# A hybrid decoder layer: the opening's VectorE and DMA work put into program order, later norms begun earlier, adaLN rows double-buffered and spread over the work, two spreads moved ahead of the FFN

## The chip, the cores and the metric

The kernel runs on one core of a Trainium2 chip. The time is device microseconds of one execution; the median of three runs of the kernel before is 2461.54 us (2461.07 to 2465.44). One more execution was profiled. The core has five engines with a queue each: TensorE (PE, with its weight loads PEld), VectorE (DVE), ScalarE (ACT), GpSimd (POOL) and SyncE (SP), whose queue issues every DMA here. Each queue is worked in order: an instruction that waits for a semaphore holds up all that stand behind it.

## The reference

One layer of a decoder with 2048 tokens and width 1024, all in float32:

```
mod = silu(c) @ w_ada + b_ada                        # adaLN: six vectors of 1024
shift1, scale1, gate1, shift2, scale2, gate2 = split(mod, 6)
h = rmsnorm(x, norm1_w) * (1 + scale1) + shift1
q, k, v, z, xbc, dt = split(h @ w_in)
a = sliding_window_attention(rope(q), rope(k), v, sinks)     # 8 heads, window 128
xbc = silu(causal_depthwise_conv(xbc, conv_w, conv_b))
y = ssd_chunked_scan(xbc, softplus(dt + dt_bias), A, ...)     # Mamba-2, chunks of 128
y = rmsnorm_by_group(y * silu(z)) * ssm_norm_w
x = x + gate1 * (concat(a, y) @ w_out)
h = rmsnorm(x, norm2_w) * (1 + scale2) + shift2
g, u = split(h @ w_gate_up);  x = x + gate2 * ((silu(g) * u) @ w_down)   # width 2816
out = rmsnorm(x, final_norm_w)
```

## The kernel before

A float32 product is made of three matmuls: each operand is split into a part `hi`, rounded to the matmul's type, and the rest `lo`, and hi·hi, hi·lo and lo·hi are summed in a PSUM bank (`mm3`, L231 to L234). So each weight and each activation that goes into a product is first split: `hi` on ScalarE, `lo` on VectorE or GpSimd (`weight`, L213; `split`). Weights of the mixer that are used in four blocks are split once and their halves stored in HBM and read again (L228, L220).

Tokens come in 4 blocks of 512 (b = 0 to 3). Activations are held with the width on the partitions, 8 tiles of 128 x 512. The layer runs in two phases. The mixer phase takes each block through `queries`, `keys_values`, `convolved` and `gated` (projections with 24 to 48 dense matmuls between two `yield`s; one such stretch is called a piece here), and `out_proj` for blocks 0 and 1. The FFN phase first multiplies two blocks at a time by the gate and up weights (`quad`, seven products instead of eight from sums of operands, which `operands` prepares), then `down`.

Between the pieces, side work is let in. `beside` calls `tick(ratio)` after each piece of the main work; each tick adds the ratio to a counter, and for each whole unit the first generator in `sides` makes one step: attention and the state-space scan of an earlier block. MIX, 1.2, is that ratio from block 1 on, and 0.5 holds in block 0 and at the end. `pending` holds things to be done after so many ticks. `finish` runs a side's remaining steps without dense work between them.

The norm of the next block is `norm1`: eight tiles of x are loaded, squared on ScalarE and added up on GpSimd (L242), then the column sums are made on TensorE (L247), the root on VectorE (`rstd`, `rsqrt`), the root is spread to all partitions by a matmul with ones (`spread`, L260), x is loaded a second time and multiplied with it (`modulated`, L265 to L268). `norm_ahead` starts this, and puts the sums 8 ticks and the spread 12 ticks later. For block 0 `first_norm` (L920) keeps x in SBUF, adds its squares on VectorE, and then multiplies out 16 rows of adaLN (`ada`: a row of 128 x 1024 is loaded and reduced against silu(c) on VectorE, L153). The rotary tables (`rope_tables`, L172) stand before it in the program.

The other 32 rows of adaLN are done in halves of 128 x 512 through one buffer `aw` (`ada_halves`, L155): load, reduce (L159), load the second half, reduce. `with_ada` lets in two rows for three pieces, from `convolved` of block 0 until `convolved` of block 1.

The order on TensorE is the program's own within the mixer phase (`manual_schedule`). On all other engines, and on SP's queue, a planner puts the instructions in an order by the times that it estimates; buffers come from pools with a fixed number each (`t` 9, `hl` 12, `raw` 5, `w` 6), and a load into a used buffer waits until the last reader is done.

## Time and profile before

| | |
|---|---|
| median of 3 runs | 2461.54 us (2461.07 to 2465.44) |
| the profiled execution: its time, its span | 2463.36 us, 2461.7 us |
| TensorE busy | 2246.5 us of the span, 91% |
| VectorE, GpSimd, ScalarE busy | 1439.6, 1255.0 and 967.5 us |
| mean granted TensorE clock | 0.963 |
| DMA | 403.81 MB, mean 164 GB/s |
| first dense matmul, keys and values of block 0, convolved of block 1 | 50.5, 80.0 and 265 us |
| first matmul of the FFN, the FFN without stalls | 813.8, from 861 us |

The span runs from the first to the last instruction. A row of the page's groups or of the waits names the engine, the tile and the line, and what ended the wait: "PE d L247 <- POOL t L242" is a matmul of L247 that waited for GpSimd's L242. The line of an operation can be a helper's. The granted clock falls where TensorE has been idle, and matmuls after an idle stretch take longer.

### The profile page before, as it was taken

The numbers are of one execution on the slowest core, as the hardware profiler recorded it, in microseconds if no ns is written. First come the engines' busy times: TensorE is split into PE (matmuls) and PEld (weight loads), VectorE is DVE, ScalarE is ACT, GpSimd is POOL, SyncE is SP. The second block draws the span as 40 slices with busy tenths as digits, with TensorE's granted clock in tenths as the row PEclk, the third lists the DMA queues.
The fourth block names the chain that finished last, engine by engine and source line by source line (L and its number), as shares of the span: only waits on it lengthen the run. The fifth ranks groups of instructions, "written<-read, shape, count | busy, mean of one in ns | idle before, by whom it ended". The sixth has DMA issues, their size and how long they took to land.

```text
span 2461.7 us, 32964 instructions
## 1 busy us (share of the span) xinstructions
PE 2246.5 (91%) x11198; PEld 1877.8 (76%) x11198; DVE 1439.6 (58%) x2526; ACT 967.5 (39%) x2004; POOL 1255.0 (51%) x1249
## 2 busy tenths in 40 slices
PE   1969789899899699999999998899799999999996
PEld 1859678787788488888888787687588888878785
DVE  8456775774334976555765533538855555554554
ACT  3444542574136543445433422224333333333332
POOL 2755633554111698654786333226766666643432
PEclk9979999999899799999999999899899999999998
DMA  5778867867876233222334654664322222263451
GB/s 228 246 266 272 297 221 246 287 221 258 272 232 195 88 116 99 82 69 86 99 99 128 217 181 152 234 205 150 133 98 77 83 85 90 78 219 99 139 163 52
DMA packets 244456, 403.81 MB, mean 164 GB/s; under 512 B 21952, under 2 KB 68032, under 8 KB 244288
## 3 DMA queue, kind: packets, MB, share of 16 engines
q1 hardware_dynamic: 243136, 400.66, 49.8%
q8 instruction: 88, 1.44, 0.2%
q10 hardware_dynamic: 1152, 1.05, 0.1%
q14 instruction: 80, 0.66, 0.1%
HBM read 307.19 MB, written 94.44 MB: 163 GB/s over the span
## 4 chain that ended last, share of the span: by engine, by line
PE 73%; DVE 7%; DMA 6%; ACT 2%; issue 1%; POOL 1%; SPq 0%; DVEq 0%; POOLq 0%; ACTq 0%
PE d L233 10%; PE d L234 10%; PE d L232 10%; PE d L794 9%; PE d L796 8%; PE d L795 8%; DMA aw<-in_wada_dram 4%; PE am L232 1%; PE am L233 1%; PE am L234 1%; DVE aw L159 1%; DVE b L770 1%; PE sm L673 1%; PE st L794 1%; PE st L796 1%
## 5 line engine op out<-in xcount | busy, mean ns | idle before, releaser
L742 ACT ACTIVATE w<-raw 128x512 fp32r<-128x512 f32 x308 | 193.8, 632 | 530.2 <-PE d L234 264.3
L794 PE MATMUL d<-b,w 128*128 128x512 f32 x924 | 373.9, 405 | 19.2 <-ACT b L769 9.4
L795 PE MATMUL d<-b,w 128*128 128x512 f32 x924 | 370.1, 401 | 1.8 <-DVE b L770 1.8
L796 PE MATMUL d<-b,w 128*128 128x512 f32 x924 | 368.9, 399 | 1.8 <-DVE w L743 1.8
L232 PE MATMUL d<-a,w 128*128 128x512 f32 (+1 forms) x720 | 280.3, 396 | 15.9 <-ACT a L862 9.6
L233 PE MATMUL d<-a,w 128*128 128x512 f32 (+1 forms) x720 | 282.1, 392 | 2.7 <-DVE a L737 2.7
L234 PE MATMUL d<-a,w 128*128 128x512 f32 (+1 forms) x720 | 282.2, 392 | 0.0
L743 POOL TENSOR_TENSOR w<-raw,w 128x512 fp32r<-128x512 f32 x88 | 118.7, 1349 | 296.2 <-ACT w L742 277.7
L743 POOL TENSOR_TENSOR w<-s,w 128x512 fp32r<-128x512 f32 x132 | 189.7, 1437 | 136.2 <-ACT w L742 123.0
L873 DVE SCALAR_TENSOR_TENSOR x<-d,mod,x 128x512 f32<-128x512 f32 (+1 forms) x182 | 131.0, 725 | 182.1 <-PE d L234 178.8
L743 DVE TENSOR_TENSOR w<-raw,w 128x512 fp32r<-128x512 f32 x220 | 194.6, 885 | 69.6 <-ACT w L742 66.9
L794 PEld LDWEIGHTS d<-b,w 128*128 128x128 f32 x924 | 175.9, 190 | 61.8 <-ACT b L769 10.9
L796 PEld LDWEIGHTS d<-b,w 128*128 128x128 f32 x924 | 176.3, 191 | 42.7 <-DVE w L743 2.3
L795 PEld LDWEIGHTS d<-b,w 128*128 128x128 f32 x924 | 176.5, 191 | 40.8 <-DVE b L770 3.8
L232 PE MATMUL d<-w,hl 128*128 128x256 f32 (+1 forms) x640 | 186.9, 292 | 2.0 <-ACT hl L267 1.6
L234 PE MATMUL d<-w,hl 128*128 128x256 f32 (+1 forms) x640 | 183.7, 287 | 3.7 <-DVE hl L268 3.7
L233 PE MATMUL d<-w,hl 128*128 128x256 f32 (+1 forms) x640 | 184.1, 288 | 0.0
L232 PEld LDWEIGHTS d<-a,w 128*128 128x128 f32 x720 | 136.5, 190 | 51.0 <-ACT a L862 12.1
L242 POOL TENSOR_TENSOR t<-t 128x512 f32<-128x512 f32 (+1 forms) x84 | 106.8, 1272 | 128.6 <-ACT t L241 121.7
L225 POOL TENSOR_TENSOR w<-raw,w 128x512 fp32r<-128x512 f32 (+1 forms) x72 | 98.3, 1373 | 129.6 <-ACT w L224 109.1
L233 PEld LDWEIGHTS d<-a,w 128*128 128x128 f32 x720 | 136.7, 190 | 36.1 <-DVE a L737 4.3
L234 PEld LDWEIGHTS d<-a,w 128*128 128x128 f32 x720 | 136.2, 189 | 30.7 <-issue 0.2
(311 smaller groups left out, 5418.4 us busy)
## 6 DMA issues: line engine op xcount, KB each, us to landing
raw<-in_wgu_dram SPq DMA_DIRECT2D x176, 256.0 KB, 2.7
raw<-in_wd_dram SPq DMA_DIRECT2D x176, 256.0 KB, 2.7
w<-w_x SPq DMA_DIRECT2D x48, 512.0 KB, 5.3
w<-w_o SPq DMA_DIRECT2D x48, 512.0 KB, 4.5
act<-t SPq DMA_DIRECT2D x88, 256.0 KB, 2.1
t<-act SPq DMA_DIRECT2D x88, 256.0 KB, 4.5
t<-in_xT_dram SPq DMA_DIRECT2D x80, 256.0 KB, 4.6
aw<-in_wada_dram SPq DMA_DIRECT2D x64, 256.0 KB, 3.5
```

The lines of the kernel that those rows point to most:

```text
L159: nc.vector.tensor_tensor_reduce(w, w, csil[:, hs], 0.5, (part if half else b_ada)[:, i:i + 1], ALU.mult, ALU.add, (mod if half else part) ...
L225: nc.gpsimd.tensor_tensor(lo, raw[:, :n], hi.bitcast(F32), ALU.subtract)
L232: nc.tensor.matmul(out, ahi, bhi, start=first, stop=False)
L233: nc.tensor.matmul(out, ahi, blo, start=False, stop=False)
L234: mm3.last = nc.tensor.matmul(out, alo, bhi, start=False, stop=last)
L242: eng.tensor_tensor(acc, acc, sq, ALU.add)
L742: nc.scalar.activation(hi, x, AF.Copy)
L743: eng.tensor_tensor(lo, x, hi.bitcast(F32), ALU.subtract)
L794: nc.tensor.matmul(out, ahi, bhi, start=first and k == 0, stop=False, skip_group_check=True)
L795: nc.tensor.matmul(out, ahi, blo, start=False, stop=False, skip_group_check=True)
L796: mm3.last = nc.tensor.matmul(out, alo, bhi, start=False, stop=k == 3, skip_group_check=True)
L873: nc.vector.scalar_tensor_tensor(x, ps, gate2[:, c:c + 1], x, ALU.mult, ALU.add)
```

## The change

The opening's VectorE, TensorE and SP instructions are put in program order (`manual_schedule` over `silu_c`, `first_norm` and `rope_tables`). In that order the norm comes first, its squares are summed by TensorE itself, each of block 0's eight tiles is modulated as soon as its two adaLN rows are there, six of the query weights are loaded between, and the rotary tables come last. The other 32 adaLN rows have two buffers `aw`; a row's two loads are issued, and its reductions come three ticks later (`ada_later`), one step at each tick, beginning with `keys_values` of block 0. The norm of block 1 is begun after `queries` of block 0, that of block 2 before `queries` of block 1, that of block 3 before `convolved` of block 2, with their sums 16 or 17 and their spreads 21 or 22 ticks later. `out_proj` of blocks 0 and 1 load and split their operands some pieces earlier (`take(out, 2)`). The attention of block 2 begins beside `keys_values` of block 3. The spreads for the FFN's first `operands` are made before `gated` of block 3, in two other banks. MIX is 1.1. In the FFN phase the attention of block 3 comes before both scans.

On VectorE in the opening there stood, in the middle of the rotary table's steps (L182 to L185) and the root (L193 to L205) of block 0's norm:

```order
L153 ISA m_352,mod<-m_352,csil,vec 128x1024
L153 ISA mod 128x1
L183 SCALAR_TENSOR_TENSOR s<-s 128x512
L194 TENSOR_SCALAR rstd<-rsq 128x4
L932 SCALAR_TENSOR_TENSOR scl_151<-mod,vec 128x1
L184 SCALAR_TENSOR_TENSOR s<-s 128x512
L204 TENSOR_TENSOR rsq<-rstd 128x4
L185 SCALAR_TENSOR_TENSOR s<-s 128x512
L205 SCALAR_TENSOR_TENSOR rsq<-rsq,ms 128x4
```

Now the root is done in one go, and after it each tile of the operand `hl` follows its two rows, with a reduction of a later adaLN row (`aw`, L165) ahead of each of its two passes:

```order
L154 ISA m_357,mod<-m_357,csil,vec 128x1024
L154 ISA mod 128x1
L948 SCALAR_TENSOR_TENSOR scl_145<-mod,vec 128x1
L165 ISA aw,part<-aw,csil,vec 128x512
L165 ISA part 128x1
L274 SCALAR_TENSOR_TENSOR t<-m_229,scl_145,at 128x512
L165 ISA aw,mod<-aw,csil,part 128x512
L165 ISA mod 128x1
L277 SCALAR_TENSOR_TENSOR hl<-t,mod,hl 128x512
```

The rows of adaLN are no longer between the root's steps; the tables have moved behind the eighth such group, and 20 halves of later rows stand ahead of the first rotary product.

In SP's queue the first reading of block 1's x (L273) stood between the weights of `convolved` (`in_wx`), the stores of their halves (L228) and other traffic (numbers behind a name tell its uses apart):

```order
L273 DMA t_903<-in_xT_dram 128x512
L228 DMA w_x_3_1_1183<-w_1178 256x1x512
L223 DMA raw_1479<-in_wx_dram 128x512
L393 DMA xs0_203<-sx_984 128x512
L478 DMA m1_2964<-kv3_190 128x256
L228 DMA w_x_4_0_1251<-w_1246 256x1x512
L223 DMA raw_1504<-in_wx_dram 128x512
L228 DMA w_x_4_1_1270<-w_1265 256x1x512
L393 DMA xs0_203<-sx_1063 128x512
L223 DMA raw_1562<-in_wx_dram 128x512
L273 DMA t_908<-in_xT_dram 128x512
```

Now it is over before the first of these stores, and adaLN loads stand between:

```order
L229 DMA raw_1042<-in_wx_dram 128x512
L282 DMA t_728<-in_xT_dram 128x512
L160 DMA aw_2322<-in_wada_dram 128x512
L160 DMA aw_2536<-in_wada_dram 128x512
L282 DMA t_733<-in_xT_dram 128x512
L160 DMA aw_2537<-in_wada_dram 128x512
L282 DMA t_738<-in_xT_dram 128x512
L160 DMA aw_2869<-in_wada_dram 128x512
L282 DMA t_743<-in_xT_dram 128x512
L160 DMA aw_2870<-in_wada_dram 128x512
L360 DMA q0_149<-m2_673 128x512
```

The x loads have moved up past 13 weights of `convolved`, and 21 halves of adaLN have come ahead of the last of them. Up to the first reloaded weight of block 1's `convolved`, SP now issues 77.1 MB with all 64 halves of `aw`, where before it issued 64.9 MB with 22 of them (counted from the shapes in the order).

The diff, cut to its core:

```diff
-MIX, RATIO_UP = 1.2, 0.6
+MIX, RATIO_UP = 1.1, 0.6
-    common, extra = tiles(sb, M1, M2, M4), tiles(xp, 4, 10, 4)
+    common, extra = tiles(sb, M1, M2, M4), tiles(xp, 3, 10, 4)
...
-    def ada_halves(i):
-        for half in range(2):
-            w, hs = big("aw", 1, pool=ip), slice(half * T, (half + 1) * T)
+    def ada_later(i):
+        halves = [slice(0, T), slice(T, D)]
+        ws = [big("aw", 2, pool=ip) for _ in halves]
+        for w, hs in zip(ws, halves):
             nc.sync.dma_start(w, wada[i, :, hs])
-            nc.vector.tensor_tensor_reduce(w, w, csil[:, hs], 0.5, (part if half else b_ada)[:, i:i + 1],
-                                           ALU.mult, ALU.add, (mod if half else part)[:, i:i + 1])
+        for _ in range(3):
+            yield
+        m, pt = mod[:, i:i + 1], part[:, i:i + 1]
+        for w, hs, src, dst in zip(ws, halves, (b_ada[:, i:i + 1], pt), (pt, m)):
+            nc.vector.tensor_tensor_reduce(w, w, csil[:, hs], 0.5, src, ALU.mult, ALU.add, dst)
+        yield
...
-    def operands(s, ops, bp, banks):
-
-        bc = [spread(y_of[2 * s + j], bc=banks[j]) for j in range(2)]
+    def operands(s, ops, bp, bc):
...
     def first_norm():
-        accs, h, x0 = [tmp(), tmp()], [], []
+        st, h, x0, ws = side_bank(0), [], [], []
         for d in range(KT):
             x = extra.m2()
             x0.append(x)
             last_load = nc.sync.dma_start(x, xT[0, d])
-            square_into(accs[d % 2], x, d < 2, nc.vector)
-        acc = accs[0]
-        nc.vector.tensor_tensor(acc, acc, accs[1], ALU.add)
-        bc = spread(rstd(acc, st=side_bank(0)), bc=side_bank(1))
+        for d in range(2):
+            ada(8 + d, common.m4)
+            ada(d, extra.m4)
         for d in range(KT):
-            ada(8 + d, common.m4)
+            sq = tmp()
+            nc.scalar.activation(sq, x0[d], AF.Square)
+            for t in range(NT):
+                nc.tensor.matmul(st[:, 2 * t:2 * t + 2], sq[:, t * P:(t + 1) * P], ones[:, 0:2],
+                                 start=d == 0 and t == 0, stop=d == KT - 1 and t == NT - 1, skip_group_check=True)
+        y = root_of(st, NT)
+        bc = spread(y, bc=side_bank(1))
+        ada(10, common.m4)
+        for d in range(KT):
             nc.vector.scalar_tensor_tensor(scl1[:, d:d + 1], mod[:, 8 + d:9 + d], 1.0, n1w[:, d:d + 1],
                                            ALU.add, ALU.mult)
-            ada(d, extra.m4)
             h.append(modulated(x0[d], bc, scl1[:, d:d + 1], sh1[:, d:d + 1], operand()))
-        return h, last_load
-
-    rope_tables()
-    h, last_load = first_norm()
+            if d + 2 < KT:
+                ada(2 + d, extra.m4)
+            if d + 3 < KT:
+                ada(11 + d, common.m4)
+            if d % 2 == 0 and d < 6:
+                ws.append([weight(wq[c][d // 2], 512, (f"q{c}", d // 2), False) for c in range(2)])
+        return h, last_load, ws
+
+    with tc.manual_schedule(engines={mybir.EngineType.PE, mybir.EngineType.DVE, mybir.EngineType.SP}):
+        for i in range(2):
+            silu_c(i)
+        h, last_load, first_ws = first_norm()
+        rope_tables()
...
     def tick(ratio):
...
+        if ada_rest:
+            next(ada_rest[0], None)
...
-        pending.extend([[8, lambda: next(g)], [12, lambda: next(g)]])
+        pending.extend([[n, lambda: next(g)] for n in at])
...
         run(queries(0, h), 0)
+        with tc.issue_after(last_load.ins):
+            nxt = norm_ahead(1, (17, 21))
+        rest = rest_of_ada()
+        ada_rest.append(rest)
         run(keys_values(0, h), 0)
...
+        nxt = norm_ahead(2, (16, 22))
+        run(queries(1, h), MIX)
...
+        nxt = norm_ahead(3, (16, 22))
         run(convolved(2, h), MIX)
         finish(mix0)
         out = out_proj(0, y_of, lambda c: operand(), lambda c: dense())
-        nxt = norm_ahead(3)
-        run(gated(2, h), MIX)
-        next(out)
-        next(out)
+        g = gated(2, h)
+        take(g, 4)
+        for _ in range(4):
+            tick(MIX)
+        take(out, 2)
+        run(g, MIX)
         run(out, MIX)
         h = nxt
         run(queries(3, h), MIX)
-        run(keys_values(3, h), MIX)
+        out = out_proj(1, y_of, lambda c: operand() if c % 2 else halved(extra.m4()), lambda c: dense())
         finish(mix1)
+        sides.append(attentions(2, common))
+        take(out, 2)
+        run(keys_values(3, h), 0.5)
         prepared(3)
...
         run(out, 0.5)
         run(convolved(3, h), 0.5)
+        bcs = [spread(y_of[b], bc=side_bank(2 + b)) for b in range(2)]
         run(gated(3, h), 0.5)
+        drain(rest)
         finish(sides[0] if sides else None)
...
+    sides.extend([attentions(3, common), ssds(2, stepping[2], common), ssds(3, stepping[3], common)])
...
-        drain(operands(0, ops, bp, [dense(), dense()]))
+        drain(operands(0, ops, bp, bcs))
```

54 lines of the change are left out of this document (17 added, 37 removed).

## The prediction

> **What bounds the kernel now.** I read the page first, then the waits of TensorE, the stretches by stage, the timeline of the opening, the adaLN tile `aw`, and last the order of both programs. The page:
>
> ```profile
> span 2461.7 us, 32964 instructions
> PE 2246.5 (91%) x11198; PEld 1877.8 (76%) x11198; DVE 1439.6 (58%) x2526; ACT 967.5 (39%) x2004; POOL 1255.0 (51%) x1249
> ...
> PE 73%; DVE 7%; DMA 6%; ACT 2%; issue 1%; POOL 1%; SPq 0%; DVEq 0%; POOLq 0%; ACTq 0%
> ```
>
> TensorE is busy for 91% of the span and carries 73% of the chain that ended last. The change adds no dense matmul and removes none, so it can only win what TensorE idles, 2461.7 - 2246.5 = 215 us, and the slow matmuls that follow idling. Where that lies, by stage (the columns are busy us and count of PE, PEld, DVE, ACT and POOL, the granted TensorE clock, the DMA share and its GB/s; the rows are four pieces of the opening, convolved of block 0, the rest up to convolved of block 1, that and the rest of its phase, the middle of the mixer, its end, and the start of the FFN):
>
> ```profile
> 10.00:15.00 5.00, 0.00 (x0) 0.00 (x0) 5.00 (x10) 4.50 (x7) 0.00 (x0) 1.00 1.05 406
> 35.00:40.00 5.00, 0.00 (x0) 0.00 (x0) 5.00 (x11) 1.15 (x2) 1.29 (x1) 1.00 0.88 327
> 45.00:50.00 5.00, 2.08 (x2) 0.50 (x2) 4.11 (x11) 0.29 (x1) 0.00 (x0) 1.00 0.00 0
> 80.00:85.00 5.00, 4.57 (x38) 4.38 (x37) 3.46 (x11) 2.36 (x4) 5.00 (x7) 1.00 0.41 121
> 92.50:176.50 84.00, 57.78 (x236) 46.39 (x235) 51.48 (x123) 43.71 (x95) 51.80 (x54) 0.82 0.85 296
> 176.50:265.30 88.80, 80.48 (x637) 78.98 (x636) 58.82 (x160) 40.73 (x108) 49.48 (x67) 0.96 0.85 287
> 265.30:350.30 85.00, 67.81 (x338) 56.34 (x337) 60.12 (x141) 44.20 (x103) 37.12 (x51) 0.90 0.75 245
> 447.20:659.10 211.90, 202.85 (x1261) 179.79 (x1258) 122.83 (x301) 101.73 (x251) 93.78 (x141) 0.98 0.77 255
> 805.00:861.00 56.00, 33.48 (x131) 24.60 (x130) 54.31 (x76) 32.39 (x73) 38.44 (x26) 0.70 0.29 90
> 861.00:1362.00 501.00, 501.00 (x2444) 417.21 (x2442) 315.80 (x466) 219.44 (x489) 350.78 (x339) 1.00 0.32 98
> ```
>
> From 861 to 1362 TensorE never stops: nothing is to be had there. What the change can reach lies before 861. Who ended the long waits:
>
> ```profile
> PE d L247 <- POOL t L242: 32.3, 2, 19.3
> PE at L260 <- DVE t L258: 27.1, 1, 27.1
> PE am L247 <- DVE t L928: 17.9, 1, 17.9
> ...
> PE d L232 <- ACT m L210: 9.4, 1, 9.4
> ...
> PE at L491 <- DMA m<-q: 4.8, 1, 4.8
> ...
> PE d L260 <- DVE t L258: 3.7, 1, 3.7
> ```
>
> The first row is the norms of blocks 1 and 2: TensorE stood at their column sums until GpSimd had added the last square. The two longest single waits are the opening's own norm. The 9.4 us are the first matmul of the second output projection, which waits for its operand to be split.
>
> **The opening, +4 us (from -8 to +14).** VectorE sets the pace there (5.00 of 5.00 us busy in the pieces at 10 and at 35, while DMA, at 406 GB/s first, has nothing left at 45). The new order lets TensorE begin as soon as the first pair of operands is there, but it puts two things ahead of the rotary tables: 12 of the 16 first adaLN rows with the modulation, and 20 halves of *later* adaLN rows. The durations:
>
> ```profile
> 15.25 0.69 DVE L185 SCALAR_TENSOR_TENSOR s<-s 128x512 f32<-128x512 f32 x1
> ...
> 22.02 0.43 DVE L181 TENSOR_SCALAR s<-s 128x512 f32<-128x512 f32 x1
> ...
> 23.70 1.28 DVE L153 CUSTOM_DVE_ANT_0 m<-m,csil,vec 128x1024 f32<-128x1024 f32 x1
> ...
> 24.39 7.78 POOL L225 TENSOR_TENSOR w<-raw,w 128x512 fp32r<-128x512 f32 x5 [18.68 <-DMA raw<-in_wq_dram]
> ...
> 24.90 1.49 DVE L182 TENSOR_SCALAR s<-s 128x512 f32<-128x512 f32 x1
> ...
> 48.93 5.36 DVE L265 SCALAR_TENSOR_TENSOR t<-m,scl,at 128x512 f32<-128x512 f32 x8 [0.90 <-PE at L260]
> ...
> 78.06 0.42 DVE L312 TENSOR_TENSOR m<-d,cos 128x256 f32<-128x256 f32 x1 [18.48 <-PE d L234]
> ...
> 79.99 0.28 PE L232 MATMUL d<-w,hl 128*128 128x264 f32 x1
> ```
>
> and of a half row of adaLN (durations are least, median and most, in ns):
>
> ```profile
> L158 SPq DMA_DIRECT2D aw<-in_wada_dram x64: 327/333/1067, 130.5 to 474.7; - x64
> L159 DVE CUSTOM_DVE_ANT_0 aw<-aw,csil,vec x32: 740/752/1667, 136.0 to 473.6; 128x512 f32<-128x512 f32 x32
> ...
> DMA to landing us min/median/max: 2.5/3.5/6.0
> ```
>
> On VectorE, in the new order, up to the first rotary product: 12 rows x 1.28 = 15.4, 20 halves x 0.75 = 15.0, 16 modulation passes x 0.67 (5.36 / 8) = 10.7, the root, its spread and the scales about 4, the tables about 8 (8 passes of 0.43 and 7 of 0.69). That is 53 us after the first four rows, which I put at about 17 us (the first x loads and four rows are 4.7 MB and land at the opening's pace of some 400 GB/s, four passes behind them): 70 us with no wait at all. To it come the weight splits on GpSimd: beside them L182 took 1.49 us where L181, its like, took 0.43, and the five splits cost VectorE some 4.5 us, 0.9 each. About ten fall into the stretch: 9 us. And the last table halves wait for loads that SP issues only after weights whose buffers TensorE frees late: I take 3. So 82, the first bank is free four short products later (1.7 us), and keys and values begin at 84 instead of 79.99. Bounds: no waits at all, 72, is -8; all 16 splits and 8 us of loads, 94, is +14. I take the middle, since the rows show the splits beside VectorE, and no row shows the new loads. The matmuls of the queries that now run early gain nothing, as TensorE waits for the tables behind them.
>
> The Trainium skill (SBUF — State Buffer, "SBUF: two separate sides") speaks against this place: a VectorE operation in a two-port mode or with two SBUF inputs, and a GpSimd one that reads SBUF, exclude each other for the whole instruction. The row agrees in kind, with 1.06 us lost (1.49 - 0.43) of a split of 1.56 (7.78 / 5); by the rule taken whole, 16 x 1.56 = 25 us would be lost instead of 9, and the sum below would be 16 us higher, an estimate near the first rival's time.
>
> **Norm of block 1, -22 us (from -17 to -24).** Its sums wait 19.3 us at 120. The eight loads of x are now issued ahead of all but three of the weights of convolved, not between their stores, and the sums stand 13 pieces deep instead of 8. With the wait goes the slow clock behind it:
>
> ```profile
> 120.00:130.00 10.00, 0.00 (x0) 0.00 (x0) 3.69 (x4) 4.42 (x7) 7.75 (x9) 0.76 1.03 384
> 130.00:140.00 10.00, 0.78 (x4) 0.79 (x4) 0.76 (x2) 2.53 (x4) 5.50 (x4) 0.50 0.56 198
> 140.00:150.00 10.00, 10.00 (x39) 8.39 (x39) 5.49 (x26) 1.31 (x3) 1.44 (x2) 0.71 0.34 108
> ```
>
> At 0.71 the ten us after it lose 2.9. I take 19.3 + 2.7.
>
> **What the adaLN rows cost there, +12 us (from 0 to +32).** Today one buffer serves 64 halves one after another:
>
> ```profile
> DVE aw L159 <- DMA aw<-in_wada_dram: 85.4, 41, 7.6
> ```
>
> From 130.5 to 474.7, a half is issued every 344.2 / 63 = 5.5 us: load, wait, product, next load; VectorE stands 85 us for it. In the new order of SP all 64 stand ahead of the first reloaded weight of block 1's convolved, where today 22 do: 42 more, 11.0 MB, and 77.1 MB in all instead of 64.9. At the 345 GB/s of saturated stretches (331, 344 and 363 in these rows) that is 32 us of transfer.
>
> ```profile
> 160.00:170.00 10.00, 5.19 (x22) 4.24 (x21) 9.11 (x17) 8.11 (x16) 5.90 (x5) 0.81 0.96 331
> 200.00:210.00 10.00, 9.18 (x78) 8.97 (x77) 4.27 (x15) 8.45 (x29) 2.53 (x2) 1.00 0.95 344
> 210.00:220.00 10.00, 8.37 (x60) 8.26 (x60) 5.00 (x12) 4.60 (x13) 4.09 (x4) 0.83 1.04 363
> ```
>
> 20 halves go into the opening, where DMA rests after 40 us. 44 remain for the stretch 92.5 to 265 instead of 22: 5.8 MB, 17 us. That stretch has 0.15 x 172.8 = 26 us of DMA to spare today, but 22 of them go with the norm's wait: 17 - 4 = 13, taken as 12. Nothing if they find their place, 32 if none of the 42 does. The second reading of block 1's x now stands behind 53 halves, so its queries feel it first.
>
> **Norm of block 2, -16.** 32.3 - 19.3 = 13.0 us, and 3 of clock as above (0.90 granted in that stage). It begins ahead of block 1's queries, and its sums stand four pieces into convolved instead of eight; from -10, if traffic delays its loads, to -18. **The mixer from 265 to 447, -5.** No adaLN load is left in it: the 4.8 us at L491 go, where SP issued a query tile behind `aw`; 0 to -12. **Spread of block 3's norm, -3** of the 3.7 us, 0 to -4. **The second output projection, -12** (-5 to -14): loads and splits now stand ahead of eight pieces of keys and values, 96 matmuls x 0.12 = 12 us, and the wait of 9.4 us goes with 3 of clock. The ratio 1.1 for 1.2 leaves enough turns: some 102 steps of the two side streams against 1.1 x 101 pieces, so nothing is drained bare.
>
> **Start of the FFN, -8** (0 to -20). VectorE is busy 54.31 of 56 us there, TensorE 33.48. The spreads are out of it, and in the new order eight passes (six products with the spread, two differences) stand ahead of the last gate: 8 x 0.7 = 5.6. Block 2's attention starts eight pieces sooner, four steps fewer are left: 2 us. The lower twelve products and all operand halves remain, since their buffers are freed only by the last gate.
>
> **The sum**: 4 - 22 + 12 - 16 - 5 - 3 - 12 - 8 = -50. The profiled execution took 2463.4 us with its span of 2461.7, the median of the runs is 2461.5, 1.8 lower. 2463.4 - 50 - 1.8 = 2411.6, say **2412**.
>
> **Rivals.** *All gains but the adaLN ones' price in full*: DMA and in-order queues eat convolved's gain, +32 instead of +12: 2432. For it: 0.85 share already. Against: rest in the opening. *Better than the sum*: opening -8, adaLN 0, FFN -20: 2461.5 - 86 = 2376. For it: 215 us of idling that sit on few causes; against: VectorE still carries the FFN's start.
>
> *Slower*: the adaLN loop stays at its 5.5 us. In an in-order queue a load behind a wait on VectorE, and a product on VectorE behind that load, hold up all that stands behind both: weights, x, rotary products. If the second buffer brings no overlap, the 44 halves left at 82 us need 44 x 5.5 = 242 us, and block 1's convolved begins at 324 instead of 265: +59 in place of the first three terms, -44 from the rest, so 2476. It decides from 5.2 us a half (82 + 44 x 5.2 = 309, 44 late). A load of 3.5 and two products of 0.75 make 5 us for two halves, with SP's own waits some 6 or 7, so it is unlikely. *No effect*: the stalls come back elsewhere, block 1's queries waiting for x as long as its norm did, and the FFN's start unchanged: about 2460.
>
> **Chances**: the sum, 0.57, its own range 2395 to 2430; adaLN's full price 0.20; better 0.13; slower 0.07; no effect 0.03. The best ends of all terms give 2361, the worst 2476; holding 8 in 10, 2376 to 2450. About 0.2%, 5 us, can be told from no change: faster 0.57 + 0.20 + 0.13 = 0.90, same 0.03, slower 0.07.
>
> **What would show it.** In the new profile: keys and values begin between 72 and 94 us, behind a wait on the rotary products; no wait of over 5 us at L253; `aw` at about 3.5 us a half and over before block 1's convolved, which begins near 257 (265.3 + 4 - 22 + 12 = 259) with a DMA share over 0.9 ahead of it; no wait of 9 us at the second projection; VectorE still full at the FFN's start. Wrong, if convolved of block 1 begins after 280, or TensorE waits over 30 us for x or the tables.

## The result, and the profile after

The changed kernel takes 2438.66 us (median of 4 runs, 2434.49 to 2439.58) where the kernel before, run beside it, takes 2463.1 (2461.07 to 2465.44). The ratio is 0.9897, 95% interval 0.988 to 0.9914. That is faster by 24 us; 50 were forecast (and 2412 us). The page after (its execution took 2434.5 us, span 2432.8), span, busy times and the chain of waits:

```profile
span 2432.8 us, 33013 instructions
...
PE 2261.8 (93%) x11254; PEld 1891.9 (78%) x11254; DVE 1461.9 (60%) x2519; ACT 967.3 (40%) x2004; POOL 1262.3 (52%) x1249
...
PE 77%; DVE 8%; DMA 5%; issue 4%; POOL 3%; ACT 3%; SPq 1%; POOLq 0%; DVEq 0%; ACTq 0%
```

TensorE's idling fell from 215 to 2432.8 - 2261.8 = 171 us, so 44 of it went; but 15 of these came back as busy time (2246.5 to 2261.8). The stretches say where. First come those of the kernel before: up to convolved of block 0, from there to the gates, from the gates to convolved of block 1, and from that to convolved of block 2 (the columns are those of the windows in the prediction):

```profile
0.00:92.40 92.40, 41.68 (x299) 39.57 (x300) 61.67 (x128) 27.76 (x45) 35.46 (x78) 1.00 0.54 196
92.40:177.20 84.80, 58.58 (x242) 47.19 (x242) 52.28 (x124) 44.41 (x96) 52.60 (x55) 0.82 0.85 295
177.20:265.30 88.10, 79.78 (x631) 78.28 (x630) 58.12 (x160) 40.03 (x107) 48.78 (x66) 0.96 0.85 288
265.30:447.90 182.60, 153.67 (x997) 140.00 (x995) 121.20 (x319) 75.47 (x191) 70.82 (x123) 0.92 0.78 251
```

And the changed kernel: a piece of the opening, all of it, the same three stretches, and the FFN's start and first half:

```profile
80.00:90.00 10.00, 0.00 (x0) 0.00 (x0) 9.90 (x16) 3.79 (x5) 6.04 (x4) 0.63 0.60 194
```

```profile
0.00:112.60 112.60, 65.09 (x355) 60.11 (x356) 88.49 (x169) 32.76 (x53) 49.80 (x84) 0.83 0.68 236
112.60:180.60 68.00, 52.75 (x240) 43.03 (x239) 47.15 (x125) 38.71 (x86) 42.49 (x47) 0.93 0.94 332
180.60:282.50 101.90, 86.08 (x629) 83.37 (x628) 76.94 (x189) 42.57 (x104) 60.39 (x62) 0.88 0.89 298
282.50:430.90 148.40, 143.09 (x962) 131.35 (x961) 93.20 (x229) 65.88 (x165) 58.96 (x119) 0.98 0.72 237
```

```profile
787.00:815.00 28.00, 14.30 (x42) 8.83 (x41) 27.63 (x31) 20.99 (x51) 23.78 (x16) 0.66 0.39 118
815.00:1332.00 517.00, 512.92 (x2483) 425.10 (x2483) 339.03 (x487) 228.24 (x505) 366.28 (x347) 0.99 0.31 96
```

Between 80 and 90 us TensorE does nothing at all, and VectorE is full. The query matmuls, which ran in one go before, are now strung along the opening at a granted clock of 0.83 in the mean: the same 192 matmuls keep TensorE busy for 35.3 us instead of 26.0. The rest of the difference between 65.1 and 41.7 us is for the most part the norm's column sums, 64 matmuls and 13.8 us at 9 to 23 us, where before there were 8 with 1.8 us. Convolved of block 0 has become 16.8 us shorter, the stretch behind it 13.8 longer, and the one from block 1 to block 2 34.2 shorter. Against the forecast, from the starts of the stages in both traces (us):

| | before | after | difference | forecast |
|---|---|---|---|---|
| start of keys and values, block 0 | 80.0 | 98.3 | +18.3 | +4 |
| keys and values, block 0 | 12.4 | 14.3 | +1.9 | 0 |
| from convolved of block 0 to that of block 1 | 172.9 | 169.9 | -3.0 | -22 + 12 = -10 |
| from there to the first output projection | 286.1 | 254.4 | -31.7 | -16 - 5 - 3 = -24 |
| from there to the last gate's end | 252.8 | 244.6 | -8.2 | -12 |
| from there to the end of the first quads | 557.6 | 548.9 | -8.7 | -8 |
| the rest of the span | 1099.9 | 1102.4 | +2.5 | 0 |
| sum | | | -28.9 | -50 |

Who waits now (TensorE, whole execution):

```profile
PE d L238 <- DVE s L322: 19.9, 2, 19.6
PE d L238 <- ACT hl L276: 14.8, 8, 2.9
PE sm L253 <- POOL t L248: 11.9, 2, 8.5
...
PE at L574 <- DVE m L578: 8.7, 4, 5.4
PE d L238 <- DVE so L411: 8.6, 2, 6.7
PE am L493 <- DMA m<-kv: 8.4, 1, 8.4
```

The long waits of the norms at their sums (L247 before, L253 now) are gone from the mixer: what is left in that group lies at 1633 and 2413 us. In their place stand one of 19.6 us on the rotary products (L322) at 79 us, and two kinds that VectorE ends, with their longest at 174 and 196 us: the attention's transposed operand (L578) and the gates' epilogue (L411, the pass that empties a bank of the gates). Convolved of block 0 has a long wait for DMA besides, 8.4 us until 126.7, at the attention's keys and values, which are read back (L493). During the wait on the gates' epilogue VectorE is nearly full, and between 170 and 283 us it stands for 10.4 us in all at loads of adaLN:

```profile
184.50:200.00 15.50, 11.28 (x94) 10.84 (x92) 14.08 (x17) 6.05 (x13) 9.52 (x8) 0.96 0.95 320
```

```profile
DVE aw L165 <- DMA aw<-in_wada_dram: 10.4, 7, 3.2
```

The opening in VectorE's and GpSimd's own rows (a timeline; us of start, us, then the instruction):

```profile
80.12 1.50 DVE L188 TENSOR_SCALAR s<-s 128x512 f32<-128x512 f32 x1
81.66 1.67 DVE L189 SCALAR_TENSOR_TENSOR s<-s 128x512 f32<-128x512 f32 x1
...
84.93 1.74 DVE L190 SCALAR_TENSOR_TENSOR s<-s 128x512 f32<-128x512 f32 x1
...
88.78 0.43 DVE L187 TENSOR_SCALAR s<-s 128x512 f32<-128x512 f32 x1
...
92.00 0.69 DVE L190 SCALAR_TENSOR_TENSOR s<-s 128x512 f32<-128x512 f32 x1
...
96.76 0.42 DVE L321 TENSOR_TENSOR m<-d,cos 128x256 f32<-128x256 f32 x1
```

```profile
79.59 3.19 POOL L231 TENSOR_TENSOR w<-raw,w 128x528 fp32r<-128x528 f32 x2
82.74 3.38 POOL L248 TENSOR_TENSOR t<-t 128x512 f32<-128x512 f32 x2
```

L190 takes 0.69 us where GpSimd rests and 1.74 where it adds or splits. The tables begin at 75.7 and end at 96.8 us: 21 us for some 8 us of their own passes and eight later adaLN halves, 6 us; six meetings with GpSimd passes add 6 us, and a wait for a half adds 1.2. Waits in the opening (to 100 us) that the forecast had no term for:

```profile
DVE m L154 <- DMA m<-in_wada_dram: 4.9, 1, 4.9
...
DVE ms L258 <- PE am L942: 3.8, 1, 3.8
...
DVE hl L277 <- ACT hl L276: 3.7, 4, 1.4
```

The tile `aw`, whose 64 loads are now over at 265 us, and what VectorE waits for it:

```profile
L160 SPq DMA_DIRECT2D aw<-in_wada_dram x64: 327/328/2020, 16.5 to 265.3; - x64
...
  DMA aw<-in_wada_dram: 19.2, 15
...
DMA to landing us min/median/max: 2.5/3.8/8.4
```

### The profile page after: what moved, and what is told of

It reads as the page before. It is cut to its first block, busy times and chain, and to the rows that moved or that the text cites. A ratio compares the mean times of both kernels' runs of the same rounds, so it can differ in the third digit from the quotient of the medians.

```text
span 2432.8 us, 33013 instructions
## 1 busy us (share of the span) xinstructions
PE 2261.8 (93%) x11254; PEld 1891.9 (78%) x11254; DVE 1461.9 (60%) x2519; ACT 967.3 (40%) x2004; POOL 1262.3 (52%) x1249
## 4 chain that ended last, share of the span: by engine, by line
PE 77%; DVE 8%; DMA 5%; issue 4%; POOL 3%; ACT 3%; SPq 1%; POOLq 0%; DVEq 0%; ACTq 0%
PE d L238 11%; PE d L240 11%; PE d L239 11%; PE d L803 8%; PE d L805 8%; PE d L804 8%; PE am L238 1%; PE am L239 1%; PE am L240 1%; POOL w L231 1%; PE at L574 1%; DMA t<-act 1%; DMA t<-in_xT_dram 1%; PE sm L683 1%; PE st L803 1%
## 5 line engine op out<-in xcount | busy, mean ns | idle before, releaser
L238 PE MATMUL d<-a,w 128*128 128x512 f32 (+1 forms) x720 | 281.1, 398 | 12.4 <-ACT a L871 11.5
L238 PE MATMUL d<-w,hl 128*128 128x256 f32 (+1 forms) x640 | 194.8, 304 | 43.3 <-DVE s L322 19.9
L240 PE MATMUL d<-w,hl 128*128 128x256 f32 (+1 forms) x640 | 190.8, 298 | 4.6 <-DVE hl L277 4.6
L239 PE MATMUL d<-w,hl 128*128 128x256 f32 (+1 forms) x640 | 189.7, 296 | 0.0
L238 PEld LDWEIGHTS d<-w,hl 128*128 128x128 f32 x640 | 130.8, 204 | 48.4 <-issue 20.9
```

The source lines that it names most:

```text
L238: nc.tensor.matmul(out, ahi, bhi, start=first, stop=False)
L239: nc.tensor.matmul(out, ahi, blo, start=False, stop=False)
L240: mm3.last = nc.tensor.matmul(out, alo, bhi, start=False, stop=last)
```

## The experiments

Three questions were open: what made the opening 14 us worse than forecast; why a removed wait of 19.3 us left the way to block 1's convolved only 3.0 us shorter; and where the rest was won. All stretches below are from the starts of the stages in each run's trace, "halves" are the halves of later adaLN rows whose products fall between convolved of block 0 and that of block 1.

| kernel | keys and values start | convolved 0 | gates 0 to convolved 1 | convolved 1 to output projection | halves | ratio to before, 95% |
|---|---|---|---|---|---|---|
| before | 80.0 | 84.8 | 88.1 | 286.1 | 23 | |
| changed | 98.3 | 68.0 | 101.9 | 254.4 | 39 | 0.9897 (0.9880 to 0.9914) |
| tables_first | 78.1 | 71.7 | 99.0 | 256.8 | 40 | 0.9839 (0.9817 to 0.9861) |
| later_rows_after_kv | 91.1 | 60.8 | 107.6 | 267.2 | 38 | 0.9937 (0.9915 to 0.9958) |
| loads_without_products | 92.1 | 65.2 | 97.5 | 252.9 | 39 | single run |
| queries_without_gpsimd | 93.2 | 67.9 | 101.2 | 252.5 | 39 | single run |
| norms_alone | 81.1 | 62.0 | 100.1 | 275.7 | 23 | 0.9971 (0.9956 to 0.9986) |
| all_rows_from_block_1 | 75.4 | 62.0 | 90.5 | 284.6 | 0 | 0.9879 (0.9848 to 0.9909) |
| rows_moved_norms_as_before | 79.5 | 81.7 | 76.6 | 304.2 | 0 | 1.0028 (1.0018 to 1.0039) |
| rows_spread_tables_last | 93.7 | 52.7 | 90.3 | 256.9 | 6 | 0.9821 (0.9804 to 0.9837) |
| rows_spread_to_the_end | 77.7 | 60.9 | 88.2 | 257.6 | 6 | 0.9772 (0.9741 to 0.9803) |
| rows_spread_again | 77.7 | 59.9 | 89.4 | 259.5 | 6 | 0.9792 (0.9775 to 0.9808) |
| norm_1_spread_sooner | 78.0 | 62.1 | 84.3 | 254.6 | 6 | 0.9758 (0.9734 to 0.9782) |
| spreads_at_the_ffn | 99.6 | 67.7 | 102.7 | 251.1 | 39 | 0.9927 (0.9902 to 0.9952) |

**tables_first.** The rotary tables ahead of the norm:

```diff
-        h, last_load, first_ws = first_norm()
-        rope_tables()
+        rope_tables()
+        h, last_load, first_ws = first_norm()
```

> The changed kernel with the rotary tables ahead of the first norm in the opening's order, nothing else by hand. In the changed kernel keys and values of block 0 begin at 98.3 us (forecast 84), behind a wait of 19.6 us on the rotary products, and block 1 loses 14 us between 180.6 and 282.5. Theory V (VectorE sets both: its own instructions, and 1.0 us more for each that meets a GpSimd pass): the 8 tables' passes fill VectorE's idling before 20 us, keys and values begin at 78 to 82 (the queries' last matmul ends at 78.7), most of that stays, 2418 to 2426. Theory D (the transfers of 112 to 282 set the pace, DMA share 0.83 to 1.02): keys and values begin at 78 to 82 too, but convolved of block 1 still begins at 278 to 283 and the time stays at 2433 to 2440.

Measured: keys and values at 78.1 us, 20.2 earlier, and 2421.85 us (2420.79 to 2423.96). VectorE's rows of this run:

```profile
9.31 0.17 DVE L179 CAST posf<-posi 128x16 f32<-128x16 int32 x1
...
17.84 0.43 DVE L192 TENSOR_SCALAR s<-s 128x512 f32<-128x512 f32 x1
18.18 1.28 DVE L154 CUSTOM_DVE_ANT_0 m<-m,csil,vec 128x1024 f32<-128x1024 f32 x1
```

The same 16 instructions, from 9.3 to 18.2 us, without one that is longer than its like, while the first rows of adaLN were still on their way (the 4.9 us of L154 above). The wait of 19.6 us is gone, TensorE goes from the last query to the keys with a break of 0.4 us, and 19.4 of the 20.2 us are still there at block 1's convolved. So it was the tables' place, as theory V says, and the transfers do not swallow it. Block 1's loss is another matter: from the gates of block 0 to convolved of block 1 it is 99.0 us here, 2.9 less than in the changed kernel, where theory V had put both down to VectorE.

**queries_without_gpsimd.** How much of the opening is GpSimd's:

```diff
-        nc.gpsimd.tensor_tensor(lo, raw[:, :n], hi.bitcast(F32), ALU.subtract)
+        if key[0] in ("q0", "q1") and not store:
+            nc.scalar.activation(lo, raw[:, :n], AF.Copy)
+        else:
+            nc.gpsimd.tensor_tensor(lo, raw[:, :n], hi.bitcast(F32), ALU.subtract)
```

> The changed kernel, but the low halves of block 0's eight query weights are copied on ScalarE instead of being subtracted on GpSimd (the split of these weights is left out). In the changed kernel's opening 16 VectorE instructions are 1.0 us longer than their like, each beside a GpSimd pass, and 7 of them beside these weights. If GpSimd is what lengthens them, these 7 have their like's duration, and keys and values begin 6 to 8 us earlier, at 90 to 92. If something else does (loads that arrive, ScalarE), at 97 to 100, and the seven stay long.

Measured: keys and values at 93.2 us, 5.1 earlier, and 2427.94 us in a single run. In the changed kernel 16 VectorE instructions of the opening are longer than their like, 15.9 us together, and each lies beside a GpSimd pass; here the seven beside the query weights have their like's duration. 11 others are long by 11.0 us together, all beside the splits of the key weights and the norm's adds, some of them new meetings, which is why 5 us are won and not 7. TensorE's own wait shows what stays, the tables at the end (line 325 is the rotary product here):

```profile
PE d L241 <- DVE s L325: 22.7, 2, 22.3
```

**later_rows_after_kv.** None of the later rows in the opening (their steps begin behind keys and values of block 0 as well):

```diff
-            nc.sync.dma_start(w, wada[i, :, hs])
+            with tc.issue_after(kv_store[0].ins):
+                nc.sync.dma_start(w, wada[i, :, hs])
```

> The changed kernel with all loads of the later adaLN rows behind the first store of keys and values of block 0, so that none of the 20 halves stands in the opening. Theory V: the opening loses 20 x 0.75 = 15 us of VectorE and 1.8 us of waits, keys and values begin at 80 to 84; the 15 us come back in part in block 1, where VectorE is busy for 0.78: convolved of block 1 begins at 268 to 275, 2422 to 2432. Theory D: the 20 halves (5.2 MB, 15 us at 345 GB/s) are carried in the full stretch instead, convolved of block 1 begins at 280 or later, 2436 to 2445.

Measured: keys and values at 91.1 us, not 80 to 84, and 2444.61 us (2443.28 to 2450.0), 6 slower than the changed kernel. Both halves of theory V's sum were off. The 12 halves between the modulation's passes had cost little, since VectorE waits there for ScalarE's high half, 0.8 us or more each time, when it has no product to fill in (8.7 us of such waits here, 3.7 in the changed kernel). And the halves taken out of the opening went behind convolved of block 1, where 26 of them made the way to the first output projection 12.8 us longer. So these 20 halves cost less in the opening than behind it.

**loads_without_products.** What of that price is VectorE's work:

```diff
-            nc.vector.tensor_tensor_reduce(w, w, csil[:, hs], 0.5, src, ALU.mult, ALU.add, dst)
+            nc.vector.tensor_tensor_reduce(w[:, 0:8], w[:, 0:8], csil[:, 0:8], 0.5, src, ALU.mult, ALU.add, dst)
```

> The changed kernel, but the products of the later adaLN rows read only 8 of the 512 columns of each half (so those rows of adaLN are left out of the computation); all their loads stay. Theory V: 20 x 0.6 = 12 us and some GpSimd meetings go from the opening, keys and values begin at 83 to 87, and block 1 gets its 14 us back: convolved of block 1 at 250 to 262, 2405 to 2418. Theory D: keys and values as by V, but the loads still set the pace: convolved of block 1 at 275 to 283, 2430 to 2440.

Measured: keys and values at 92.1, convolved of block 1 at 269.8, 2422.98 us (a single run). Keys and values are missed by both theories (83 to 87); convolved of block 1 and the time lie between the two. With 39 halves of loads and next to no product, 162.7 us from convolved of block 0 to that of block 1 instead of 169.9: the products are 7.2 us of it. What is left over the 152.5 of the run without any half (below, with the tables first), 10.2 us, is put down to the loads and the waits for them; VectorE's 10.4 us at such loads in the changed kernel fit that.

**norms_alone.** The kernel before with the norms of blocks 1 and 2 moved, and nothing else:

```diff
+        with tc.issue_after(last_load.ins):
+            nxt = norm_ahead(1, (17, 21))
         run(keys_values(0, h), 0)
...
-        with tc.issue_after(last_load.ins):
-            nxt = norm_ahead(1)
...
+        nxt = norm_ahead(2, (16, 22))
         run(with_ada(queries(1, h)), MIX)
...
-        nxt = norm_ahead(2)
```

> The kernel before with only the norms of blocks 1 and 2 begun at the new places (sums 17 and 16, spreads 21 and 22 ticks later); opening, adaLN rows, projections and FFN as before. Theory V of the forecast: the two waits of 32.3 us and some 6 of clock go, 2420 to 2428. Rival S (the stall only hid traffic: DMA share 1.03 at 120 to 130 us): the time comes back as waits for weights and for the second reading of x, 2440 to 2452.

Measured: 2455.54 us (2448.39 to 2460.63), some 7 us where 38 were forecast for these two terms; its profiled execution, the fastest of ten, has a span 15.0 us shorter, so the stretches here are at the good end. Convolved of block 0 falls by 22.8 us, about all that the wait and its clock had cost. Ahead of it 3.0 us are lost (it begins at 95.4 instead of 92.4), and the stretch behind it grows by 12.0. The planner also let the loop of later rows begin at 67 us instead of 130, so seven halves more lie ahead of convolved of block 0. From the trace of this run (windows, then VectorE's group of the norm's first multiplication, then TensorE's waits from 92 to 560 us):

```profile
95.40:157.40 62.00, 52.47 (x240) 42.67 (x239) 44.60 (x112) 38.65 (x86) 40.37 (x47) 0.94 0.98 342
157.40:257.50 100.10, 86.14 (x634) 84.10 (x633) 65.87 (x167) 45.60 (x114) 61.69 (x72) 0.90 0.86 281
```

```profile
L265 DVE SCALAR_TENSOR_TENSOR t<-t,scl,d 128x512 f32<-128x512 f32 x8 | 5.9, 741 | 7.7 <-DMA t<-in_xT_dram 6.4 <-PE d L260 1.3
```

```profile
PE at L564 <- DVE m L568: 11.9, 3, 6.2
PE d L232 <- DVE so L401: 10.3, 2, 5.2
...
PE st L661 <- DVE m L654: 5.6, 1, 5.6
```

The multiplications of block 1's norm now all stand among the gates' epilogues; before, five of the eight began ahead of the gates. Two of them wait for their second reading of x (3.1 us until 184.6 and 3.3 until 204.9), and what stands behind them in VectorE's queue waits with them. TensorE waits 10.3 us for banks that the epilogues free, until 178.9 and until 200.1. One of the readings lies ahead of the second of these waits and none ahead of the first, so the readings are a part of the price and not all of it. Block 2's norm falls into this stretch too, with its first eight loads (202.8 to 228.7 us) and GpSimd's seven adds, which before came behind convolved of block 1; no run separates the two norms. Convolved of block 1 to that of block 2 is 6.8 us shorter, not 16, with new waits in the list (L564, L661).

**all_rows_from_block_1.** tables_first, and every later row behind block 1's last store of keys and values:

```diff
-            nc.sync.dma_start(w, wada[i, :, hs])
+            with tc.issue_after(kv_store[7].ins):
+                nc.sync.dma_start(w, wada[i, :, hs])
...
         prepared(1)
+        rest = rest_of_ada()
+        ada_rest.append(rest)
```

> The kernel with the tables first (2421.9), and all 64 halves of the later adaLN rows behind the last store of keys and values of block 1, so none in the opening nor between convolved of block 0 and convolved of block 1. In the runs so far convolved of block 1 takes 63.6 us with no half in it, 69.0 with 6 and 74.4 with 20, and the products are only a part of that. Theory T (a half costs some 0.5 us wherever DMA is over 0.7, whatever queue it stands in): from convolved of block 0 to that of block 1 145 to 152 us instead of 170.7, but 254 + 64 x 0.5 = 286 from there to the first output projection, 2420 to 2432 in all. Theory P (it is the place between block 0's stores and block 1's loads that costs): the first stretch the same, the second 256 to 265, 2398 to 2408.

Measured: 2431.4 us (2425.98 to 2437.58). 152.5 us between the two convolved instead of 170.7, and 284.6 behind instead of 256.8: 18.2 us for 40 halves, 0.46 each, are won, and with 64 halves there the way behind is 30.2 us longer than the changed kernel's 254.4 without any, 0.47 each. Theory T holds, P falls. Without any half VectorE still waits 8.8 us for second readings of x among the gates, and TensorE 9.7 for their epilogues.

**rows_moved_norms_as_before.** The kernel before with its norms as they were and no later row before convolved of block 1 (the loop of one buffer begins there):

```diff
-        run(with_ada(convolved(0, h)), 0.5)
-        run(with_ada(gated(0, h)), 0.5)
+        run(convolved(0, h), 0.5)
+        run(gated(0, h), 0.5)
...
-            with tc.issue_after(after_load.ins):
+            with tc.issue_after(kv_store[7].ins):
                 ada_halves(i)
```

> The kernel before with its norms where they were, but no later adaLN row before convolved of block 1 (loads behind block 1's last keys and values, the loop of one buffer as before, from there up to the last gate). From convolved of block 0 to that of block 1 the kernel before takes 172.9 us with 23 halves and 22 us of norm wait and slow clock; with the norms moved 162.1 with 23, 169.9 with 39, and without the waits 152.5 with none. Theory H (the norm's wait hid the rows, so each half costs 0.5 us only once the wait is gone): 168 to 174 here, nothing won by their absence. Theory R (each half costs 0.5 us with the wait too): 158 to 164. The end goes with it: H 2455 to 2475, R 2445 to 2455.

Measured: 2468.44 us (2466.53 to 2473.71), slower, but the stretch in question takes 158.3 us, as theory R says: 14.6 us less for 23 halves. So theory H falls; the norm's wait had not hidden the rows. The end is H's number only because the way behind, with 18 halves more, is 18.1 us longer (304.2 instead of 286.1), a row that neither theory had priced. That is no price per half: 6.9 of the 18.1 us lie between convolved of block 1 and that of block 2, where there are 36 halves instead of 35. The gates and keys of this run are what that stretch takes when nothing disturbs it:

```profile
91.90:173.60 81.70, 57.67 (x243) 46.51 (x242) 44.87 (x106) 44.45 (x96) 49.16 (x54) 0.83 0.79 276
173.60:250.20 76.60, 76.00 (x632) 75.34 (x630) 44.57 (x131) 40.60 (x108) 47.79 (x67) 1.00 0.83 281
```

Here TensorE is full at a granted clock of 1.00, in 76.6 us. With the norms moved and still no half it takes 90.5 (all_rows_from_block_1). So the moved norms (block 1's multiplications, and block 2's first loads and squares) cost that stretch 13.9 us without any row in it, and 12.0 with 13 and 16 halves in it (88.1 to 100.1): a price beside that of the rows.

**rows_spread_to_the_end** and **rows_spread_tables_last.** Six later rows in the opening, the other 26 one every five ticks, each held to the store of its place; with the tables first and with the tables last:

```diff
+            with ExitStack() as stack:
+                if after is not None:
+                    stack.enter_context(tc.issue_after(after.ins))
+                nc.sync.dma_start(w, wada[i, :, hs])
...
-        for i in (*range(16, 24), *range(32, 40), *range(24, 32), *range(40, 48)):
-            yield from ada_later(i)
+        for n, i in enumerate((*range(16, 24), *range(32, 40), *range(24, 32), *range(40, 48))):
+            yield from ada_later(i, None if n < 6 else stores[-1])
+            for _ in range(0 if n < 6 else 1):
+                yield
```

> The kernel with the tables first (2421.9), six later rows in the opening as there, the other 26 one every five ticks up to the last gate, each held back to the store of its place. Theory T with a price that falls to nothing where DMA has room: about 8 halves instead of 46 between the two convolved, so 18 to 20 us less there; the 44 that go behind cost at most 0.5 us each in the 150 us where DMA is over 0.75, so 10 at most: 2405 to 2416. Theory T with the same price everywhere: 2418 to 2424. Theory P: 2398 to 2404.

> The changed kernel with only its later adaLN rows spread out (six in the opening, then one every five ticks, each held back to the store of its place); the rotary tables stay last in the opening. The tables alone were worth 17 us, both together 32. If the two add, 15 us here: keys and values at 94 to 97, 148 to 153 us from convolved of block 0 to that of block 1 instead of 169.9, 2418 to 2428. If the spread rows only paid because the tables' move had left them room, the stretch stays above 160 and the time is 2430 to 2438.

Measured: 2406.91 us (2397.33 to 2410.12) and 2417.36 us (2414.13 to 2418.5). The first is inside the range of theory T with a falling price; the second is just below its range, with a stretch 5 us shorter than expected. The stretch between the two convolved takes 149.1 and 143.0 us: 34 and 33 halves less than in tables_first and the changed kernel are worth 21.6 and 26.9 us, 0.6 and 0.8 each. With 24 halves in it the stretch behind is only 3.2 and 2.5 us longer than the changed kernel's (0.1 a half; 5.1 us, 0.2 a half, in the repeat below), but the 22 that fall behind the first output projection make the way to the last gate 8 us longer (252.7, after 244.6), 0.4 a half, though they come as singly. So the price per half is not one number, and it goes by the stretch; that spreading as such lowers it is not shown. By the medians the spread rows alone give 21 us, the tables alone 17, both 32; by the ratios to the kernel before on the same chip 19, 14 and 31 (26 in the repeat), so whether they add is open.

**norm_1_spread_sooner** and **rows_spread_again.** Against the wait that took the norm's place, the first of these has the norm's sums and spread a few ticks sooner; the second is rows_spread_to_the_end once more, on the same chip:

```diff
-            nxt = norm_ahead(1, (17, 21))
+            nxt = norm_ahead(1, (13, 16))
```

> The kernel with the tables first and the rows spread to the end (2406.9), with the norm of block 1's sums 13 and its spread 16 ticks after its start instead of 17 and 21; its squares were added by 121.6 us there and the sums came at 139.3, so nothing waits for them. From the gates of block 0 to convolved of block 1 that kernel takes 88.2 us, the kernel before without rows there 76.6 at full clock. Theory W (VectorE's multiplications of the norm wait for the second reading of x, some 7 us in all, and the gates' passes of L414 stand behind them, so TensorE waits 8.5 us for two of them, and the clock falls): the readings come 15 us sooner, the two waits shrink below 3 us, 78 to 84 us, 2396 to 2403. Theory D: the readings only push other transfers back, the same 86 to 90 us, 2404 to 2410.

> The kernel with the tables first and the rows spread to the end once more, beside the run above on the same chip: 2403 to 2410, as it was (2406.9).

Measured: 2400.34 us (2393.91 to 2406.98) and 2409.98 us (2408.6 to 2412.4). Gates to convolved: 84.3 us, and 89.4 in the second. TensorE's waits from 75 to 245 us, of the second and then of the first:

```profile
PE d L241 <- DVE so L414: 9.9, 2, 6.7
PE am L241 <- DVE k_ring L500: 2.4, 1, 2.4
```

```profile
PE d L241 <- DVE so L414: 5.4, 2, 4.5
PE am L241 <- DVE k_ring L500: 5.2, 1, 5.2
```

The wait on the gates' epilogue shrinks as theory W says, but to 5.4 us and not below 3, and 2.8 of the gain are paid back by the attention's keys in convolved of block 0. VectorE's own waits for the second reading of x fall from 8.8 to 0.8 us in that stretch, so what is left of TensorE's wait has another cause. Only 2.9 of the 11 us between the two profiled executions are won between the two convolved; 5.0 lie behind, up to the first output projection, which theory W does not cover. The two intervals just touch (0.9734 to 0.9782, and 0.9775 to 0.9808): likely the fastest, by some 10 us, but not beyond doubt. Of all kernels here it is 1.4% faster than the changed one.

**spreads_at_the_ffn.** The changed kernel with the two spreads at the FFN's start again:

```diff
-        bcs = [spread(y_of[b], bc=side_bank(2 + b)) for b in range(2)]
...
-        drain(operands(0, ops, bp, bcs))
+        drain(operands(0, ops, bp, [spread(y_of[j], bc=dense()) for j in range(2)]))
```

> The changed kernel with the two spreads made at the FFN's start again, in the main banks, as in the kernel before. The forecast gave 8 us to the FFN's start, 5.6 of them for eight VectorE passes done before the last gate; the start measured 8.7 less. If the passes ahead are what it is, 5 to 8 us more between the last gate and the end of the first quads, 2443 to 2447. If it is the order of the side streams (attention of block 2 begun sooner), 0 to 2 us, 2437 to 2441.

Measured: 2443.2 us (2441.28 to 2445.97; ratio 0.9927, 0.9902 to 0.9952, not clear of the changed kernel's interval), and from the last gate's end to that of the first quads 554.0 us instead of 548.9. The 50 us from the last gate's end, of this run and of the changed kernel:

```profile
779.50:829.50 50.00, 26.24 (x106) 18.61 (x105) 48.16 (x64) 30.30 (x69) 35.12 (x25) 0.66 0.36 108
```

```profile
781.50:831.50 50.00, 32.91 (x131) 22.82 (x131) 47.66 (x59) 33.14 (x75) 38.45 (x26) 0.73 0.31 98
```

VectorE is nearly full in both; with the passes made beforehand TensorE gets 25 more matmuls and 6.7 us more work done in it.

## Why the prediction was right or wrong

**Which way: right. How much: half.** The kernel is faster, and inside the range of 2376 to 2450, but the size is half of the forecast: -24 us for -50 in the medians, -28.9 in the profiled executions. One of the forecast's own signs of being wrong came true, convolved of block 1 after 280 us (282.5), and keys and values begin at 98.3, outside the 72 to 94 that it named. Two steps failed, the opening and the worth of the norms' waits, and they were wrong by more than the end shows, since one line of the table came out better than forecast by some 8 us. The nearest rival in number, "adaLN's price in full" (2432), is not what happened: the rows' price was not the largest error.

**The opening, the step that failed most: +18.3, forecast +4 with at most +14.** The sum put the first rotary products at 82 us; they came at 96.8. The terms that it had were near: 20 halves, 12 rows, the root. It left out what an in-order VectorE waits for others: 3.8 us for the column sums, now on TensorE, and 3.7 for ScalarE's high halves; the first four rows were done at 19.1 us, not 17; and the meetings with GpSimd cost 15.9 us, not 9. The 0.9 us a meeting was below its own row: the five splits there lengthened five instructions by 5.4 us, 1.07 each, not 4.5. These are 3.8 + 3.7 + 2.1 + 6.9 = 16.5 us; the loads were waited for 1.2 less than I had added and the root took 0.8 less, which leaves 14.5 of the 14.8. The choice of the middle, and an upper end that allowed only the splits and the loads to be late, were wrong: waits between engines had no place in it. That TensorE would wait for the tables, behind the rotary products, was forecast and is what the trace shows. What should have been asked is whether something else could go where VectorE stands, and it stood idle for some 9 of its first 14 us: tables_first gets 20.2 us back with one exchanged line.

The meetings measured 15.9 us, in 16 instructions of VectorE, and all 16 lie beside a GpSimd pass of 1.3 us or more. Each begins while the pass runs, fifteen of them with 1.1 to 1.3 us of it left, and these lose about 1.0 us, even one over 128x1 (L948, 1.20 us instead of 0.15); the one with 0.76 us left (L277 at 59.1) loses 0.57. So the number of meetings and the rest of the pass that is met make the cost here, not the length of the split taken whole. By the rule of the Trainium skill that the forecast weighed (SBUF — State Buffer, "SBUF: two separate sides"), taken whole, the estimate was 25 us instead of 9; the trace agrees with it in kind, and lies between the two in size.

**Norms of blocks 1 and 2, -22 and -16: the wait was read rightly, its worth was not.** The 19.3 us with their clock did go, 22.8 in convolved of block 0. But norms_alone gives only 10.8 us between the two convolved, 3.0 of which are lost again ahead of them, and 6.8 by that of block 2: 14.6 instead of 38. The step that failed is "I take 19.3 + 2.7": it took the wait away and left the norm's 16 VectorE passes and eight readings without a place. They now stand among the gates, with the gates' epilogues behind them: 12.0 us in that stretch. The sentence that block 1's second reading stands behind 53 halves and is felt first came near it, but carried no number; and even without any half the stretch pays 13.9 us. What holds VectorE up there differs by kernel. Where few or no halves are in the stretch, it is in part the late reading: norm_1_spread_sooner takes VectorE's waits for it from 8.8 to 0.8 us and TensorE's wait on the epilogue from 9.9 to 5.4. In the changed kernel itself the norm's first multiplication (L274) never waits in that stretch (0.0 us of idle time before its eight passes): there the epilogue of the 6.7 us wait stands behind VectorE's own work, six passes of it lengthened by some 1 us each beside GpSimd, and later VectorE waits 10.4 us for adaLN loads. How the 13.9 us divide between the norm of block 1 and the start of that of block 2 stays open.

**adaLN rows, +12: the price per half was about right for this stretch, the account had one side only.** The forecast charged some 0.5 us a half for 22 more of them. The runs give 0.46 (tables_first against all_rows_from_block_1), and from norms_alone to the changed kernel 7.8 us for 16 more. But 41 halves left the way from convolved of block 1 to the output projection, and for these it credited 5 us. The same price gives 19; from norms_alone to the changed kernel the stretch is 21.3 us shorter, with 34 halves less. This is why that line of the table is better than forecast by 8 us although norm 2 gave less. The forecast's reason, DMA at 345 GB/s, explains it in part only: 7.2 us in the stretch are the products and 10.2 are put down to the loads and the waits for them, and the price differs by stretch (0.1 to 0.8 us a half in the runs here). A good part of it can be named in the changed kernel: the wait of 8.4 us at L493, for which the forecast had no term. It is 6.9 to 8.7 us in the five runs that issue the rows as the changed kernel does or a little later (8.7 in loads_without_products, so it is the loads and not the products), 4.2 in norms_alone, and at most 2.8 in all others.

**Second output projection, -12: -8.2** up to the last gate, 4 short; its wait of 9.4 us on the operand's split is gone from the list, as forecast. **Start of the FFN, -8: -8.7**, with VectorE full there as forecast; spreads_at_the_ffn puts 5.1 of it on the passes made beforehand, forecast 5.6. **The mixer's other waits and the spread of block 3's norm** cannot be told apart in one line of the table.

**The rivals.** The adaLN loop does not stay at 5.5 us: 64 halves are issued in 249 us, every 3.9 us, against 3.5 forecast. Its slower mechanism, an in-order queue in which a wait holds up all that stands behind, was the right one at another place: VectorE's queue, where TensorE's epilogues and operands stand behind its waits for loads and for ScalarE.

## What to carry to other kernels

A wait that is removed is worth what the engines behind it do not then wait for: before taking its length, write down where the work that was waited for, and the work that was done during the wait, will stand in each in-order queue. When background work is moved, charge it where it goes and credit it where it leaves, each at a price measured in that stretch: here it was 0.1 to 0.8 us for the same piece. When an engine's own passes set the pace, add the waits for its partners between them, and look first for a stretch where it stands idle: work with hardly any inputs, such as tables, belongs there.

## What the hardware showed that was not expected

A VectorE instruction whose operands all lie in SBUF and that begins while a GpSimd pass runs is about 1.0 us longer whatever its own length: 0.15 to 1.20 us (128x1), 0.43 to 1.50 (128x512), 1.28 to 2.30 (128x1024). In the opening 16 of 16 lengthened instructions lie beside a GpSimd pass, and between 112 and 282 us 26 of 26 (some 22 us). The converse does not hold for all: between 10 and 282 us of the changed kernel 80 VectorE instructions with an operand in PSUM begin in the same way during a GpSimd `tensor_tensor`, such as the rotary product at 97.8 us (0.41 us), and none is longer by more than 0.02 us; of 53 others 47 are longer by over 0.2.

A background load of 256 KB with its product of 0.75 us has no fixed price in TensorE's time: 18.2 us for 40 (0.46 each) between the two convolved, 21.6 and 26.9 us for 34 and 33 when the rest of the rows are spread, 2.5 to 5.1 us for 24 behind convolved of block 1 and 8 us for 22 behind the first output projection. What sets it is known in part only: TensorE's wait of 8.4 us for a read (L493) is one part, and the rest no run here separates.
